# Turning the attention probabilities with VectorE and a trip through DRAM instead of on TensorE, in a decoder block on one core

## The chip, the core and the metric

The kernel runs on one core of one Trainium2 chip. The core has TensorE (PE in the profile: products, and PEld: loading of the stationary operand), VectorE (DVE), ScalarE (ACT), GpSimd (POOL), the queue of SyncE (SP) that issues nearly all transfers, and 16 DMA engines that carry them. Products land in PSUM, eight banks of 128 x 512 float32. The metric is the time of one execution on the device in microseconds (us), as the median of several executions.

## The reference, cut to what matters

One layer for 256 tokens of width 1024: a SwiGLU feed-forward, a mixing layer of two branches, a second SwiGLU feed-forward, a norm. The change lies in the mixing layer, between the softmax and the branch projections:

```python
n = rmsnorm(h, mix_norm[l])
z = n @ w_in[l]                                  # q, k, v (8 heads of 64) and two gMLP parts of 512
p_own = softmax(logits)                          # causal, 256 keys: one block holds the sequence
attn = einsum('bhqp,bhpd->bhqd', p_own, v_own)   # probabilities times values, by head
y_attn = attn @ w_branch_attn[l]
y_gmlp = gm @ w_branch_gmlp[l]                   # gm: spatial gating of the other branch
gates = sigmoid(n @ w_gate[l] + b_gate[l])       # 2048 columns
merged = gates[..., :D] * y_attn + gates[..., D:] * y_gmlp
h = h + merged @ w_out[l]
```

## The kernel before, in words

Activations lie with features on the partitions and the 256 tokens along the row. Each float32 weight is split into a high and a low part (`split`, lines 211 to 215: ScalarE casts, L212, VectorE subtracts, L214), and each product runs as high x both parts of the activation (L162, 512 columns) and low x high (L167, 256 columns). Weights arrive in halves of 512 KB, `raw`, in a ring of seven; SP issues the load of a half as soon as VectorE's subtraction has freed the slot seven halves earlier (L137). The split weights `w` lie in a ring of four units. A unit is split three units ahead of its use.

TensorE and SP keep the order of the code. The order of VectorE and ScalarE is set by a scheduler outside the few stretches that are marked by hand; the stretch of this change is not marked.

After the projections of q, k and the gMLP part come the scores. TensorE computes them for the two query tiles j of 128 tokens (`sc`, L586), then the spatial products of the gMLP branch (`mix`, L571, which read `gv` as stationary operand), and goes on without a break to sixteen gate blocks f = 0 to 15 (`gate_block`; the title of the change counts blocks from 1). Each is 16 products of 512 columns and 8 of 256 into one bank `pgate`; `collect` (lines 202 to 209) then copies the right half to `lo` on ScalarE (L205) and adds it to the left on VectorE (L209, output `gz`), which frees the bank. Under the gate blocks VectorE and ScalarE do the softmax of both query tiles: maxima (L596), exponentials with sums (L601), reciprocals (L604), products with the reciprocal (L606). The probabilities `prob[0]` and `prob[1]` lie with queries on the partitions, in the tile that the profile calls `mixed`; for products with the values the keys must be on the partitions.

`turn` (called behind f = 7 and f = 10, each for four heads) does that on TensorE: twelve transposes of 128 x 128 against the identity (`pk`, L634 to L636), copied from PSUM to `pT` by ScalarE (L640, two) and VectorE (L642, one). `attend` (behind f = 10 and f = 13, two head pairs each) multiplies with the values (`po`, L651 and L653) and splits the result into `aoT` for the branch projection (`pb`, L198 to L200), which begins after f = 15. Under the first four blocks `gated` finishes the gMLP branch: L659 adds the bias to a `mix` bank, L662 multiplies, and `split` writes `gmT`.

The eight banks are handed out in a row that the program fixes when it is built: gate block f takes a bank whose earlier owner must have been read out, and TensorE waits on that reader.

Later in the kernel, at L715, L723 and L727, the residual `h` is already turned as the change now turns the probabilities: VectorE transposes squares of 32 (`squares`), four transfers of 256 KB write them to DRAM (`hd`), two of 512 KB bring them back (`ht`).

Of the kernel before, what the change touches and what calls it, by code (L numbers as in the profile page):

```python
# [10 lines left out]
F32 = mybir.dt.float32  # L11
# [7 lines left out]
P = 128  # L19
D = 1024  # L20
S = 256
NT = S // P
DFF = 2816
KB = D // P
FB = DFF // P
HEADS = 8
HD = 64
# [16 lines left out]
def block_kernel(ctx, tc, t, out):  # L44
    nc = tc.nc
# [4 lines left out]
    act = ctx.enter_context(tc.tile_pool(name="act", bufs=1))  # L50
    tmp = ctx.enter_context(tc.tile_pool(name="tmp", bufs=2))
    small = ctx.enter_context(tc.tile_pool(name="small", bufs=4))
    psum = ctx.enter_context(tc.tile_pool(name="psum", bufs=8, space=PSUM))
    dram = ctx.enter_context(tc.tile_pool(name="dram", bufs=1, space=bass.MemoryType.DRAM))

    def bank(name):
        return psum.tile([P, 512], F32, tag="ps", name=name)
# [3 lines left out]
    h = act.tile([P, KB, S], F32, tag="h", name="h")  # L61
# [15 lines left out]
    ident = consts.tile([P, P], F32, name="ident")  # L77
# [133 lines left out]
    def split(hi, lo, src, later=False):  # L211
        nc.scalar.copy(hi, src)  # L212
        def rest():
            nc.vector.tensor_sub(lo, src, hi.bitcast(F32))  # L214
        return rest if later else rest()

    def alloc_T(name, tags):

        return [act.tile([P, 4, 2, S], F32R, tag=tag, name=f"{name}{c}") for c, tag in enumerate(tags)]
# [170 lines left out]
    def products(i0, nT, name, f, gu=None, ahead=ALONE):  # L390
        if gu is None:
            gu = tmp.tile([P, 2, S], F32, tag="gu", name=f"gu{name}{f}")
        w = unit(i0 + f, ahead)
        ps = [bank(f"{name}{'gu'[i]}{f}") for i in range(2)]
        by_passes([(ps[i], weights_of(w, nT, i)) for i in range(2)])
        for i in range(2):
            collect(gu[:, i, :], ps[i])
        return gu
# [50 lines left out]
    first = act.tile([P, 4, 2, S], F32, tag="nD", name="first")  # L449
# [3 lines left out]
    ps = {(f, i): bank(f"f1_{f}{i}") for f, i in at}  # L453
# [59 lines left out]
    with in_order():  # L513
# [6 lines left out]
        mix_a, mix_b = mixed[:, :FB], mixed[:, FB:]  # L520
        gates = mix_a[:, :2 * KB, :]
        gv = mix_a[:, 2 * KB:2 * KB + 4, :].rearrange("p (j a) t -> p j (a t)", j=NT)
        va = mix_b[:, 0:4, :].rearrange("p (j a) t -> p j (a t)", j=NT)
# [5 lines left out]
        prob = [mix_b[:, 8:12, :].rearrange("p a (b n) -> p (a b) n", b=2), mix_b[:, 12:20, :]]  # L529
# [36 lines left out]
    def spatial(ps, gp):  # L566

        for j in range(NT):
            for a in range(2):
                g = 2 * gp + a  # L570
                nc.tensor.matmul(ps[a * HD:(a + 1) * HD, j * P:(j + 1) * P],  # L571
                                 gv[:, j, g * HD:(g + 1) * HD], wsT[:, g, :], start=True, stop=True)


    for j in range(NT):
        n = (j + 1) * P
        per = 512 // n
        pr = prob[j]
        pr2 = pr.rearrange("p (a two) n -> p a two n", two=2)
        for a0 in range(0, HEADS // 2, per):  # L580

            pair = [bank(f"sc{j}{a0}{two}") for two in range(2)]
            for a in range(per):
                for two in range(2):
                    r = slice(two * HD, (two + 1) * HD)
                    nc.tensor.matmul(pair[two][:, a * n:(a + 1) * n], qT[r, a0 + a, j * P:(j + 1) * P],  # L586
                                     kT[r, a0 + a, :n], start=True, stop=True)
            for two in range(2):
                ps = pair[two].rearrange("p (a n) -> p a n", a=per)
                to = pr2[:, a0:a0 + per, two, :]  # L590
                if j:
                    nc.scalar.copy(to[:, :, :n - P], ps[:, :, :n - P])
                nc.vector.tensor_add(to[:, :, n - P:], ps[:, :, n - P:],
                                     mask[:, None, :].to_broadcast([P, per, P]))
        mx = small.tile([P, HEADS], F32, tag="mx", name=f"mx{j}")
        nc.vector.tensor_reduce(mx, pr, axis=AX.X, op=ALU.max)  # L596
        nm = small.tile([P, HEADS], F32, tag="nm", name=f"nm{j}")
        nc.vector.tensor_scalar(nm, mx, -(HD ** -0.5), None, op0=ALU.mult)
        sm = small.tile([P, HEADS], F32, tag="sm", name=f"sm{j}")
        for hd in range(HEADS):  # L600
            nc.scalar.activation(pr[:, hd, :], pr[:, hd, :], AF.Exp, bias=nm[:, hd:hd + 1],  # L601
                                 scale=HD ** -0.5, accum_out=sm[:, hd:hd + 1])
        ri = small.tile([P, HEADS], F32, tag="ri", name=f"ri{j}")
        nc.vector.reciprocal(ri, sm)  # L604
        for hd in range(HEADS):
            nc.vector.tensor_scalar(pr[:, hd, :], pr[:, hd, :], ri[:, hd:hd + 1], None, op0=ALU.mult)  # L606


    mix = []
    for pair in range(2):  # L610
        ps = bank(f"mix{pair}")
        for q in range(2):
            mix.append(ps[:, q * S:(q + 1) * S])
            spatial(mix[-1], 2 * pair + q)

    def gate_block(f):
        gz = tmp.tile([P, S], F32, tag="s", name=f"gz{f}")
        collect(gz, by_weights(f"pgate{f}", mg + f // 2, nT2, f % 2))  # L620
        nc.vector.tensor_mul(gz, gz, rows2)
        nc.scalar.activation(gates[:, f, :], gz, AF.Sigmoid, bias=bgate[:, f:f + 1])

    aoT, gmT = alloc_T("ag", ("nC", "nD"))

    def turn(first):

        hps = range(first, first + 2)
        pk0, pk1 = [bank(f"pk0{hp}") for hp in hps], bank(f"pk1{first}")
        for hp in hps:  # L630
            for a in range(2):
                hd, c1 = 2 * hp + a, (2 * (hp - first) + a) * P
                ps = pk0[hp - first]
                nc.tensor.transpose(ps[:, a * S:a * S + P], prob[0][:, hd, :], ident)  # L634
                nc.tensor.transpose(ps[:, a * S + P:a * S + S], prob[1][:, hd, :P], ident)
                nc.tensor.transpose(pk1[:, c1:c1 + P], prob[1][:, hd, P:], ident)  # L636
        t0 = []
        for hp, ps in zip(hps, pk0):
            t0.append(tmp.tile([P, 512], F32, tag="hg", name=f"pT0{hp}"))
            nc.scalar.copy(t0[-1], ps)  # L640
        t1 = tmp.tile([P, 512], F32, tag="gu", name=f"pT1{first}")
        nc.vector.tensor_copy(t1, pk1)  # L642
        return {hp: (t0[q], t1[:, q * S:(q + 1) * S]) for q, hp in enumerate(hps)}

    def attend(hp, t0, t1):

        po = bank(f"po{hp}")
        for a in range(2):
            hd = 2 * hp + a
            r = slice(a * HD, (a + 1) * HD)  # L650
            nc.tensor.matmul(po[r, :S], va[:, 0, hd * HD:(hd + 1) * HD], t0[:, a * S:(a + 1) * S],  # L651
                             start=True, stop=False)
            nc.tensor.matmul(po[r, P:S], va[:, 1, hd * HD:(hd + 1) * HD], t1[:, a * P:(a + 1) * P],  # L653
                             start=False, stop=True)
        split(aoT[:, hp, 0, :], aoT[:, hp, 1, :], po[:, :S])

    def gated(gp):
        m = tmp.tile([P, NT, P], F32, tag="s", name=f"mixb{gp}")
        nc.vector.tensor_add(m, mix[gp].rearrange("p (j i) -> p j i", j=NT),  # L659
                             bs[:, gp:gp + 1, :].to_broadcast([P, NT, P]))  # L660
        m2 = tmp.tile([P, S], F32, tag="us", name=f"gm{gp}")
        nc.vector.tensor_mul(m2, m.rearrange("p j i -> p (j i)"), uT[:, gp, :])  # L662
        split(gmT[:, gp, 0, :], gmT[:, gp, 1, :], m2)


    for f in range(2 * KB):
        gate_block(f)
        if f < 4:
            gated(f)
        if f == 7:  # L670
            turned = turn(0)
        elif f == 10:
            for hp in range(2):
                attend(hp, *turned[hp])
            turned = turn(2)
        elif f == 13:
            for hp in range(2, 4):
                attend(hp, *turned[hp])


    mT = alloc_T("mg", ("nA", "nB"))
    for f in range(KB):
        i = mb + 2 * (f // 4)
        ps = bank(f"pb{f}")
        c = slice(f % 4 * P, (f % 4 + 1) * P)
# [14 lines left out]
    with in_order():  # L700
# [3 lines left out]
        first = act.tile([P, 3, 2, S], F32, tag="nA", name="first2")  # L704
        gu = [products(f2, nT3, "f2", f, first[:, f]) for f in range(2)]
# [11 lines left out]
    hd = dram.tile([S, D], F32, name="hd")  # L717
# [117 lines left out]
```

## Time and profile before

| what | value |
|---|---|
| median of 3 runs | 538.11 us (538.0 to 538.14) |
| the profiled execution | 538.72 us, of it 536.8 us in the span of the profile |
| busy over the span | PE 98%, PEld 86%, DVE 76%, ACT 56%, POOL 3% |
| DMA engines | 59% busy, 194 GB/s |
| gate blocks to the first branch product (251.02 to 301.59 us) | PE 50.57 us of 50.57, DVE 42.84, ACT 38.50, DMA share 0.49 |

A busy share says only that instructions ran; what bounds a stretch is read from the waits and from the chain that ended last. A product's recorded duration is longer than its distance from the next one, because products overlap in the array: what a group costs TensorE is read from the distance between starts. In the timeline a row stands for a run of like instructions: its start, how long the run took, the engine, the line, the operation and the count; what stands in brackets is idle time ahead of it.

### The profile page before, as it was taken

What the parts mean: (1) busy time and instruction counts of PE and PEld (TensorE: products, weight loads), DVE (VectorE), ACT (ScalarE), POOL (GpSimd) and SP (SyncE); (2) the same over time, 40 slices, a digit from 0 to 9 for tenths busy, and PEclk for the clock granted to TensorE, in tenths of its full rate; (3) what the DMA queues carried; (4) which work ended last, traced back from release to release, by engine and by line L of the source; (5) the groups of instructions that cost most, each with busy time, mean ns of one, the idle gap of its engine ahead of it and who ended that gap; (6) DMA issues with size and microseconds to landing.
All of it is one profiled execution on the core that took longest, in us unless ns stands there. A gap on an engine that the chain in (4) does not pass through costs nothing.

```text
span 536.8 us, 8141 instructions
## 1 busy us (share of the span) xinstructions
PE 528.8 (98%) x3049; PEld 463.5 (86%) x3049; DVE 405.9 (76%) x682; ACT 303.0 (56%) x534; POOL 17.7 (3%) x23
## 2 busy tenths in 40 slices
PE   8999999999999999999999999999999999999995
PEld 7888888888888888888888998888888888888884
DVE  6799998788443689978897787799898878854324
ACT  7768566565433367447886544476657656553402
POOL 0040000000000001000000000001000000000002
PEclk9999999999999999999999999999999999999998
DMA  8985765657756329764266545259588765565002
GB/s 319 396 286 178 253 224 187 197 195 218 230 170 203 103 86 322 258 210 147 80 196 203 172 135 182 96 174 315 165 268 292 235 197 197 178 214 177 20 1 79
DMA packets 31287, 104.10 MB, mean 194 GB/s; under 512 B 3472, under 2 KB 6032, under 8 KB 31248
## 3 DMA queue, kind: packets, MB, share of 16 engines
q1 hardware_dynamic: 30960, 103.25, 58.2%
q8 instruction: 24, 0.39, 0.3%
q10 hardware_dynamic: 288, 0.33, 0.2%
q14 instruction: 15, 0.12, 0.1%
HBM read 101.47 MB, written 2.10 MB: 193 GB/s over the span
## 4 chain that ended last, share of the span: by engine, by line
PE 97%; DMA 1%; DVE 0%; issue 0%; ACT 0%; POOLq 0%; DVEq 0%; POOL 0%; ACTq 0%
PE acc L162 10%; PE f2u L162 7%; PE f2g L162 7%; PE f1u L162 7%; PE f1g L162 7%; PE pgate L162 6%; PE acc L167 5%; PE f2u L167 4%; PE f2g L167 4%; PE f1u L167 4%; PE f1g L167 4%; PE acch L200 4%; PE acch L198 4%; PE acch L199 4%; PE pgate L167 3%; PE pq L162 3%
## 5 line engine op out<-in xcount | busy, mean ns | idle before, releaser
L214 DVE TENSOR_TENSOR w<-raw,w 128x1024 fp32r<-128x1024 f32 x180 | 219.3, 1238 | 53.4 <-ACT w L212 53.0
L212 ACT CAST w<-raw 128x1024 fp32r<-128x1024 f32 x180 | 181.8, 1057 | 59.3 <-PE acc L167 21.2
L162 PE MATMUL f2g<-n,w 128*128 128x512 f32 x176 | 68.8, 391 | 0.0
L162 PE MATMUL f2u<-n,w 128*128 128x512 f32 x176 | 68.8, 391 | 0.0
L162 PE MATMUL f1g<-n,w 128*128 128x512 f32 x160 | 62.6, 391 | 0.0
L162 PE MATMUL f1u<-n,w 128*128 128x512 f32 x160 | 62.5, 391 | 0.0
L162 PE MATMUL acc<-f1h,w 128*128 128x512 f32 x176 | 43.4, 391 | 0.0
L167 PE MATMUL f2u<-n,w 128*128 128x256 f32 x176 | 43.2, 283 | 0.0
L167 PE MATMUL f2g<-n,w 128*128 128x256 f32 x176 | 43.0, 282 | 0.0
L167 PE MATMUL f1u<-n,w 128*128 128x256 f32 x160 | 39.2, 283 | 0.0
L167 PE MATMUL f1g<-n,w 128*128 128x256 f32 x160 | 39.1, 282 | 0.0
L162 PEld LDWEIGHTS f2u<-n,w 128*128 128x128 f32 x176 | 33.1, 188 | 6.3
L162 PEld LDWEIGHTS f2g<-n,w 128*128 128x128 f32 x176 | 33.1, 188 | 6.1
L162 PEld LDWEIGHTS acc<-f1h,w 128*128 128x128 f32 x176 | 31.9, 188 | 5.8
L162 PEld LDWEIGHTS f1u<-n,w 128*128 128x128 f32 x160 | 30.1, 188 | 5.7
L162 PEld LDWEIGHTS f1g<-n,w 128*128 128x128 f32 x160 | 30.1, 188 | 5.6
L167 PEld LDWEIGHTS f2u<-n,w 128*128 128x128 f32 x176 | 33.7, 191 | 0.9
L167 PEld LDWEIGHTS f2g<-n,w 128*128 128x128 f32 x176 | 33.6, 191 | 0.9
L162 PE MATMUL pgate<-n,w 128*128 128x512 f32 x128 | 33.1, 396 | 0.0
L199 PE MATMUL acch<-w,f2h 128*128 128x512 f32 x84 | 32.7, 389 | 0.0
L200 PE MATMUL acch<-w,f2h 128*128 128x512 f32 x84 | 32.7, 389 | 0.0
L198 PE MATMUL acch<-w,f2h 128*128 128x512 f32 x84 | 32.7, 389 | 0.0
(191 smaller groups left out, 933.0 us busy)
## 6 DMA issues: line engine op xcount, KB each, us to landing
raw<-in_f SPq DMA_DIRECT2D x84, 512.0 KB, 5.1
raw<-in_f1d SPq DMA_DIRECT2D x22, 512.0 KB, 4.4
raw<-in_f2d SPq DMA_DIRECT2D x22, 512.0 KB, 3.9
raw<-in_gate SPq DMA_DIRECT2D x16, 512.0 KB, 4.6
raw<-in_qk SPq DMA_DIRECT2D x8, 512.0 KB, 5.4
raw<-in_out SPq DMA_DIRECT2D x8, 512.0 KB, 4.4
front<-in_first SPq DMA_DIRECT2D x7, 384.0 KB, 5.9
raw<-in_v SPq DMA_DIRECT2D x4, 512.0 KB, 4.5
```

The lines of the kernel that those rows point to most:

```text
L162: nc.tensor.matmul(ps, st, both.rearrange("p two n -> p (two n)"), start=first, stop=last)
L167: nc.tensor.matmul(ps[:, n:], st, both[:, 0, :], start=False, stop=False)
L198: nc.tensor.matmul(ps, sh, mh, start=first, stop=False)
L199: nc.tensor.matmul(ps, sh, ml, start=False, stop=False)
L200: nc.tensor.matmul(ps, sl, mh, start=False, stop=last)
L212: nc.scalar.copy(hi, src)
L214: nc.vector.tensor_sub(lo, src, hi.bitcast(F32))
```

## The change

The twelve-by-two transposes on TensorE and their copies go. The code of the spatial products moves ahead of the softmax, since `turned[0]` takes over the space of `gv`, which those products read; TensorE's order of scores, spatial products and gate block 0 stays. Behind the multiplication with the reciprocals, VectorE turns the probabilities in squares of 32, for all eight heads in one instruction of 128 x 256: four for query tile 0, eight for query tile 1. A square has its keys on 32 partitions then, but in the wrong band of partitions; `to_keys` (behind f = 1) writes them to DRAM by key with eight transfers, four of 128 KB and four of 256 KB, in runs of 1 KB, and `by_keys` (behind f = 4) reads three blocks of 128 keys back with 512 KB each, over the place of the probabilities. `attend` for all four head pairs stands behind f = 12; its moving operand is no longer a contiguous row but 8 (or 4) runs of 32 columns, 256 columns apart.

```diff
     for j in range(NT):
...
+        turned.append(mix_a[:, 2 * KB:2 * KB + 4, :] if j == 0 else
+                      act.tile([P, KB, S], F32, tag="nC", name="turned1"))
+        for kb in range(n // 32):
+            nc.vector.transpose(turned[j][:, kb, :].rearrange("p (h c) -> p h c", c=32),
+                                pr[:, :, kb * 32:(kb + 1) * 32])
...
-    def turn(first):
...
-                nc.tensor.transpose(ps[:, a * S:a * S + P], prob[0][:, hd, :], ident)
-                nc.tensor.transpose(ps[:, a * S + P:a * S + S], prob[1][:, hd, :P], ident)
-                nc.tensor.transpose(pk1[:, c1:c1 + P], prob[1][:, hd, P:], ident)
...
-            nc.scalar.copy(t0[-1], ps)
...
-        nc.vector.tensor_copy(t1, pk1)
...
+    gmT, = alloc_T("gm", ("nD",))
+    on_way = [dram.tile([(j + 1) * P, 4, S], F32, name=f"on_way{j}") for j in range(NT)]
+
+    def to_keys(j):
+
+        for b in range(4):
+            nc.sync.dma_start(on_way[j][:, b, :].rearrange("(k r) n -> r k n", r=32),
+                              turned[j][32 * b:32 * (b + 1)])
+
+    def by_keys():
+
+
+        for j, t0, b0 in ((0, 0, 8), (1, 0, 12), (1, 1, 16)):
+            nc.sync.dma_start(mix_b[:, b0:b0 + 4, :], on_way[j][t0 * P:(t0 + 1) * P])
...
-            nc.tensor.matmul(po[r, :S], va[:, 0, hd * HD:(hd + 1) * HD], t0[:, a * S:(a + 1) * S],
+            r, c = slice(a * HD, (a + 1) * HD), slice(hd * 32, (hd + 1) * 32)
+            nc.tensor.matmul(po[r, :S], va[:, 0, hd * HD:(hd + 1) * HD], mix_b[:, 8:16, c],
...
+            nc.tensor.matmul(po[r, P:S], va[:, 1, hd * HD:(hd + 1) * HD], mix_b[:, 16:20, c],
...
-        if f == 7:
-            turned = turn(0)
-        elif f == 10:
-            for hp in range(2):
-                attend(hp, *turned[hp])
-            turned = turn(2)
-        elif f == 13:
-            for hp in range(2, 4):
-                attend(hp, *turned[hp])
+        if f == 1:
+            for j in range(NT):
+                to_keys(j)
+        elif f == 4:
+            by_keys()
+        elif f == 12:
+            aoT, = alloc_T("ao", ("nC",))
+            for hp in range(4):
+                attend(hp)
```

VectorE under the first gate blocks, before: from the softmax of query tile 1 to the collect of gate block 1 (`gz1`). Numbers behind names are buffers; `w47` is the weight unit of gate blocks 8 and 9.

```order
L606 TENSOR_SCALAR mixed_2086<-mixed_2086,ri1_2581 128x256 x8
L209 TENSOR_TENSOR gz0_2611<-pgate0_2612,lo_2638 128x256
L659 TENSOR_TENSOR mixb0_2643<-mix0_2591,bs_1495 128x256
L621 TENSOR_TENSOR gz0_2611<-gz0_2611,rowsb2_2163 128x256
L662 TENSOR_TENSOR gm0_2645<-mixb0_2643,mixed_2086 128x256
L214 TENSOR_TENSOR w47_2680<-raw47_0_2338,w47_2680 128x4x256
L209 TENSOR_TENSOR gz1_2649<-pgate1_2650,lo_2667 128x256
```

The same place after (line numbers of the changed kernel), from the softmax of query tile 0:

```order
L618 TENSOR_SCALAR mixed_2086<-mixed_2086,ri0_2576 128x128 x8
L624 STREAM_TRANSPOSE mixed_2086<-mixed_2086 128x256 x4
L616 RECIPROCAL ri1_2603<-sm1_2594 128x8
L618 TENSOR_SCALAR mixed_2086<-mixed_2086,ri1_2603 128x256 x8
L209 TENSOR_TENSOR gz0_2625<-pgate0_2626,lo_2652 128x256
L624 STREAM_TRANSPOSE turned1_2613<-mixed_2086 128x256 x8
L632 TENSOR_TENSOR gz0_2625<-gz0_2625,rowsb2_2163 128x256
L664 TENSOR_TENSOR mixb0_2657<-mix0_2545,bs_1495 128x256
L214 TENSOR_TENSOR w47_2702<-raw47_0_2338,w47_2702 128x4x256
L667 TENSOR_TENSOR gm0_2659<-mixb0_2657,mixed_2086 128x256
L214 TENSOR_TENSOR w47_2702<-raw47_1_2408,w47_2702 128x4x256
L214 TENSOR_TENSOR gm0_2622<-gm0_2659,gm0_2622 128x256
L209 TENSOR_TENSOR gz1_2663<-pgate1_2664,lo_2681 128x256
```

Four transposes stand ahead of the second reciprocal; eight stand between the collects of gate blocks 0 and 1, and a subtraction of `w47` and one of `gm0` have also come ahead of `gz1`. In both programs gate block 7 takes the bank of gate block 1, so TensorE can't start it before that collect.

The queue of SP, before: loads of the weight halves (`ba` and `bg` are the branch projections).

```order
L137 DMA raw50_0_2620<-in_gate 128x1024
L137 DMA raw50_1_2683<-in_gate 128x1024
L137 DMA raw51_0_2687<-in_ba 128x1024
L137 DMA raw51_1_2750<-in_ba 128x1024
L137 DMA raw52_0_2754<-in_bg 128x1024
```

After:

```order
L137 DMA raw50_0_2634<-in_gate 128x1024
L641 DMA on_way0_2623<-mixed_2086 32x4x256 x4
L641 DMA on_way1_2624<-turned1_2613 32x8x256 x4
L137 DMA raw50_1_2705<-in_gate 128x1024
L137 DMA raw51_0_2709<-in_ba 128x1024
L137 DMA raw51_1_2772<-in_ba 128x1024
L137 DMA raw52_0_2776<-in_bg 128x1024
L648 DMA mixed_2086<-on_way0_2623 128x1024
L648 DMA mixed_2086<-on_way1_2624 128x1024 x2
L137 DMA raw52_1_2830<-in_bg 128x1024
```

The eight writes stand ahead of the second half of unit 50 (gate blocks 14 and 15) and wait for VectorE's transposes; the three reads stand ahead of the second half of unit 52 and wait for the writes to land.

## Rows read from the trace of the kernel before

**Rows 1.** The page: its first line, TensorE's clock in 40 slices, and the chain that ended last by engine.

```profile
span 536.8 us, 8141 instructions
...
PEclk9999999999999999999999999999999999999998
...
PE 97%; DMA 1%; DVE 0%; issue 0%; ACT 0%; POOLq 0%; DVEq 0%; POOL 0%; ACTq 0%
```

**Rows 2.** Who waited for whom, TensorE alone, over the whole span: us in total, times, longest.

```profile
PE warm L92 <- DVE zeros L89: 1.2, 1, 1.2
PE f L191 <- ACT n L421: 0.4, 1, 0.4
```

**Rows 3.** Timeline of TensorE's weight loads from gate block f = 6 to f = 8, with the first group of transposes between f = 7 and f = 8. The loads of L167 mark the same point in each gate block.

```profile
269.31 1.13 PEld L167 LDWEIGHTS pgate<-n,w 128*128 128x128 f32 x8
270.36 1.70 PEld L162 LDWEIGHTS pgate<-n,w 128*128 128x128 f32 x8
272.10 1.13 PEld L167 LDWEIGHTS pgate<-n,w 128*128 128x128 f32 x8
273.16 0.19 PEld L162 LDWEIGHTS pgate<-n,w 128*128 128x128 f32 x1
273.29 0.14 PEld L634 LDWEIGHTS pk<-ident,mixed 128*128 128x128 f32 x1
...
274.71 1.46 PEld L162 LDWEIGHTS pgate<-n,w 128*128 128x128 f32 x7
276.21 1.13 PEld L167 LDWEIGHTS pgate<-n,w 128*128 128x128 f32 x8
```

**Rows 4.** The same view from f = 10 to f = 11, with four heads' products and the second group of transposes between them.

```profile
281.79 1.13 PEld L167 LDWEIGHTS pgate<-n,w 128*128 128x128 f32 x8
...
283.29 0.20 PEld L651 LDWEIGHTS po<-pT,mixed 128*64 128x64 f32 x4 [0.24 <-issue]
...
284.79 0.14 PEld L634 LDWEIGHTS pk<-ident,mixed 128*128 128x128 f32 x1 [0.17 <-issue]
...
286.05 1.45 PEld L162 LDWEIGHTS pgate<-n,w 128*128 128x128 f32 x7
287.54 1.13 PEld L167 LDWEIGHTS pgate<-n,w 128*128 128x128 f32 x8
```

**Rows 5.** The same view from f = 13 to f = 14, with the other four heads' products between them.

```profile
293.13 1.13 PEld L167 LDWEIGHTS pgate<-n,w 128*128 128x128 f32 x8
...
294.62 0.20 PEld L651 LDWEIGHTS po<-pT,mixed 128*64 128x64 f32 x4 [0.25 <-issue]
...
296.12 1.46 PEld L162 LDWEIGHTS pgate<-n,w 128*128 128x128 f32 x7 [0.17 <-issue]
297.62 1.13 PEld L167 LDWEIGHTS pgate<-n,w 128*128 128x128 f32 x8
```

**Rows 6.** Groups of instructions by line and shape: count, busy us in all and mean ns of one, idle us ahead of them.

```profile
L167 PE MATMUL pgate<-n,w 128*128 128x256 f32 x128 | 17.8, 282 | 0.0
...
L640 ACT COPY pT<-pk 128x512 f32<-128x512 f32 x4 | 2.2, 583 | 0.0
...
L191 PE MATMUL f<-n,w 128*128 128x256 f32 x8 | 2.0, 431 | 0.4 <-ACT n L421 0.4
...
L642 DVE COPY pT<-pk 128x512 f32<-128x512 f32 x2 | 1.4, 689 | 0.0
```

**Rows 7.** Timeline of VectorE under gate blocks 2 to 5: the end of the softmax and the collects of gate blocks 0 and 1 (the two rows of L209).

```profile
260.50 0.20 DVE L604 RECIPROCAL ri<-sm 128x8 f32<-128x8 f32 x1 [2.40 <-ACT mixed L601]
260.74 2.19 DVE L606 TENSOR_SCALAR mixed<-mixed,ri 128x256 f32<-128x256 f32 x8
262.85 0.42 DVE L209 TENSOR_TENSOR gz<-pgate,lo 128x256 f32<-128x256 f32 x1
263.18 0.41 DVE L659 TENSOR_TENSOR mixb<-mix,bs 128x256 f32<-128x256 f32 x1
...
264.18 1.22 DVE L214 TENSOR_TENSOR w<-raw,w 128x1024 fp32r<-128x1024 f32 x1
265.31 0.42 DVE L209 TENSOR_TENSOR gz<-pgate,lo 128x256 f32<-128x256 f32 x1
```

**Rows 8.** Timeline of VectorE later in the kernel, where it turns squares of 32 of `h`: input of 8 runs of 32 elements, 256 apart.

```profile
370.77 0.76 DVE L715 STREAM_TRANSPOSE squares<-h 128x256 f32<-128x256 f32 x2
371.46 0.65 DVE L383 TENSOR_TENSOR first<-first,rowsb 128x512 f32<-128x512 f32 x1
```

**Rows 9.** Transfers. Timeline of SP's queue where it issues the writes to `hd`; then, from the views of the single lines, the issue of the four writes (ns min/median/max) with the us to their landing, the us to landing of the two reads `ht`, and that of all weight halves (L137); last, SP's row of seven loads of gate weights.

```profile
386.50 3.06 SPq L723 DMA_DIRECT2D hd<-squares  x4
...
L723 SPq DMA_DIRECT2D hd<-squares x4: 333/624/1337, 386.5 to 388.2; - x4
...
DMA to landing us min/median/max: 2.9/4.2/5.2
...
DMA to landing us min/median/max: 5.5/6.0/6.4
...
DMA to landing us min/median/max: 3.6/4.8/12.0
...
237.85 27.90 SPq L137 DMA_DIRECT2D raw<-in_gate  x7
```

**Rows 10.** Busy time of each engine from gate block 0 to the first branch product: PE, PEld, DVE, ACT, POOL (with instructions), granted clock, DMA share, GB/s.

```profile
251.02:301.59 50.57, 50.57 (x314) 44.05 (x312) 42.84 (x88) 38.50 (x90) 0.00 (x0) 1.00 0.49 156
```

More of the change, by code (lines that the diff above doesn't have):

```diff
@@ L594, in block_kernel @@
                                      mask[:, None, :].to_broadcast([P, per, P]))
+    mix = []
+    for pair in range(2):
+        ps = bank(f"mix{pair}")
+        for q in range(2):
+            mix.append(ps[:, q * S:(q + 1) * S])
+            spatial(mix[-1], 2 * pair + q)
+    turned = []
+    for j in range(NT):
+        n, pr = (j + 1) * P, prob[j]
         mx = small.tile([P, HEADS], F32, tag="mx", name=f"mx{j}")
@@ L606, in block_kernel @@
             nc.vector.tensor_scalar(pr[:, hd, :], pr[:, hd, :], ri[:, hd:hd + 1], None, op0=ALU.mult)
[L609 to L614, printed above, removed]
+        turned.append(mix_a[:, 2 * KB:2 * KB + 4, :] if j == 0 else
[3 more added lines that the diff above has]
+                                pr[:, :, kb * 32:(kb + 1) * 32])
     def gate_block(f):
@@ L622, in gate_block, with attend @@
         nc.scalar.activation(gates[:, f, :], gz, AF.Sigmoid, bias=bgate[:, f:f + 1])
-    aoT, gmT = alloc_T("ag", ("nC", "nD"))
-    def turn(first):
[L628 to L633, printed above, removed]
-                nc.tensor.transpose(ps[:, a * S:a * S + P], prob[0][:, hd, :], ident)
-                nc.tensor.transpose(ps[:, a * S + P:a * S + S], prob[1][:, hd, :P], ident)
-                nc.tensor.transpose(pk1[:, c1:c1 + P], prob[1][:, hd, P:], ident)
-        t0 = []
-        for hp, ps in zip(hps, pk0):
-            t0.append(tmp.tile([P, 512], F32, tag="hg", name=f"pT0{hp}"))
-            nc.scalar.copy(t0[-1], ps)
-        t1 = tmp.tile([P, 512], F32, tag="gu", name=f"pT1{first}")
-        nc.vector.tensor_copy(t1, pk1)
-        return {hp: (t0[q], t1[:, q * S:(q + 1) * S]) for q, hp in enumerate(hps)}
-    def attend(hp, t0, t1):
+    gmT, = alloc_T("gm", ("nD",))
[7 more added lines that the diff above has]
+            nc.sync.dma_start(mix_b[:, b0:b0 + 4, :], on_way[j][t0 * P:(t0 + 1) * P])
+    def attend(hp):
         po = bank(f"po{hp}")
@@ L649, in attend @@
             hd = 2 * hp + a
-            r = slice(a * HD, (a + 1) * HD)
-            nc.tensor.matmul(po[r, :S], va[:, 0, hd * HD:(hd + 1) * HD], t0[:, a * S:(a + 1) * S],
+            r, c = slice(a * HD, (a + 1) * HD), slice(hd * 32, (hd + 1) * 32)
+            nc.tensor.matmul(po[r, :S], va[:, 0, hd * HD:(hd + 1) * HD], mix_b[:, 8:16, c],
                              start=True, stop=False)
-            nc.tensor.matmul(po[r, P:S], va[:, 1, hd * HD:(hd + 1) * HD], t1[:, a * P:(a + 1) * P],
+            nc.tensor.matmul(po[r, P:S], va[:, 1, hd * HD:(hd + 1) * HD], mix_b[:, 16:20, c],
                              start=False, stop=True)
@@ L669, in block_kernel @@
             gated(f)
-        if f == 7:
-            turned = turn(0)
-        elif f == 10:
-            for hp in range(2):
-                attend(hp, *turned[hp])
-            turned = turn(2)
-        elif f == 13:
-            for hp in range(2, 4):
-                attend(hp, *turned[hp])
+        if f == 1:
+            for j in range(NT):
+                to_keys(j)
[5 more added lines that the diff above has]
+                attend(hp)
     mT = alloc_T("mg", ("nA", "nB"))
```

## The prediction

> **What bounds the kernel now.** I read the chain that ended last first, then TensorE's waits, then the stretch of the change. [...] From gate block 0 to the first branch product it is busy for 50.57 of 50.57 us, beside 42.84 us of VectorE and a DMA share of 0.49 [rows 10]. So a microsecond of work taken off TensorE there shortens the kernel by as much, as long as nothing that feeds TensorE comes later than TensorE now asks for it; and work put on VectorE or the DMA engines costs nothing until it is late at one of TensorE's waits.
>
> **What leaves TensorE.** In undisturbed gate blocks the loads of L167 stand 272.10 - 269.31 = 2.79 us apart [rows 3]. Across the first group of transposes they stand 276.21 - 272.10 = 4.11 apart: it costs 1.32 us, 0.11 for each of twelve (the recorded durations overlap). Across four heads' products and the second group it is 287.54 - 281.79 = 5.75, so 2.96 more than a block [rows 4]; across the other four heads' products 297.62 - 293.13 = 4.49, so 1.70 more [rows 5]. Together 1.32 + 2.96 + 1.70 = 5.98 us. What stays is the products of eight heads in one group. Two groups by their own cost are 2 x 1.70 = 3.40; of each, some 0.4 is the switch in and out (the idle times of 0.25 and 0.17 in rows 5), and a joined group has that once, which gives 3.0. [...] The gain on TensorE is then 5.98 - 3.2 = **2.8 us**, 2.6 to 3.0 between the ends.
>
> The transposes' copies go too: 4 x 0.583 us of ScalarE and 2 x 0.689 of VectorE [rows 6]. Neither engine ends the chain, so this is worth nothing by itself.
>
> By rows 3 a transpose of 128 x 128 costs 0.11 us of the one engine that never waits; by rows 8 VectorE turns twice as many elements in 0.345 us, on an engine with idle time. [...]
>
> **What the products cost.** Their number and shapes stay, but the moving operand is read in runs of 32 columns. No row shows TensorE streaming so. The nearest is VectorE, which read the same shape of runs at L715: two in 371.46 - 370.77 = 0.69 us [rows 8], as fast as its contiguous rows, 263.18 - 262.85 = 0.33 each [rows 7]. A gain is excluded, since the columns stay as many. For the upper end I take the slowest 256-column product of the trace against the usual one, 431 against 282 ns, 1.53 times [rows 6]; that one met data as it arrived. The ends are +0 and +0.53 x 3.2 = +1.7 us; I take 0, by the nearer row. [...]
>
> **What VectorE gets.** Twelve transposes at 0.345 us (rows 8) are 4.1 us, less 1.4 of copies. Four of them come behind the first softmax multiplication, in the 2.40 us in which VectorE waited for the second softmax [rows 7]: 1.4 us, hidden. The other eight come between the collects of gate blocks 0 and 1, and that is **the close place**: gate block 7 uses the bank of gate block 1. From the start of `gz0` at 262.85 to `gz1`, by the order after and the distances of rows 7: `gz0` 0.33; eight transposes 2.76; two small ones 0.66; `w47` 1.13; `gm0` 0.33; `w47` 1.13; the low part of `gm0` 0.33. The sum is 6.67, so `gz1` starts at 269.52 instead of 265.31 and ends at 269.94. TensorE began block 7 one load after 270.36, at 270.57 [rows 3]. So 0.63 us are left. If nothing overlapped (0.42 for each small instruction and transpose, 1.22 for each half of a weight) the sum is 0.42 x 13 + 2 x 1.22 = 7.90, `gz1` ends at 271.17, and TensorE waits 0.60. I take no wait; the distances are measured. ScalarE's two casts of `w47` are unmoved ahead of this, so VectorE need not wait for it. Behind `gz1` there is more room: `gz2` comes after four small instructions and a half of a weight, at 269.52 + 4 x 0.33 + 1.13 = 271.97, done by 272.4, and block 9 needs its bank at 270.57 + 2 x 2.79 = 276.15.
>
> **What SP gets.** The writes wait for the last transpose, at 262.85 + 0.33 + 2.76 + 0.08 = 266.0. I count eight issues as the four of rows 9 twice, 6 us at the most, but those for query tile 0 are free from 260 on; so the last are out by 266.0 + 3.06 = 269.1, and land by 269.1 + 5.2 = 274.3. Queued behind them is first the second half of unit 50. Before, SP issued the last gate load by 237.85 + 27.90 = 265.75 [rows 9]; now some 4 us later, for gate block 14, which began at 296.12 [rows 5]. The slowest load of the trace took 12.0 us to land, so this costs nothing. The reads stand behind the first half of unit 52, whose slot is freed by the second half of `w48`, at 271.97 + 4 x 0.33 + 1.2 = 274.5, when the writes have landed: issued by 275.8, landed by 275.8 + 6.4 = 282.2. TensorE comes to the products behind f = 12 at 270.57 + 6 x 2.79 = 287.31. That leaves **5.1 us**; with the slowest landing of the trace, 12.0, the data come at 287.8 and TensorE waits 0.5. The traffic grows by 3 MB on 156 GB/s x 50.57 us = 7.9 MB, so the share of 0.49 becomes about 0.68, and the loads have the slack named above. I count nothing. The branch projection asks for the split results three gate blocks later, where it had two.
>
> **The sum.** The profiled execution took 538.72 us, 536.8 in its span. Less 2.8 the span is 534.0. The median of the runs is 538.11, 0.61 below the profiled one, and the change lies in the middle of the span, so I take the same 2.8 from it: **535.3 us**.
>
> **Rivals.**
>
> *VectorE is late at gate block 7.* For it: VectorE is the busiest engine beside TensorE, and 0.63 us is little. Against it: the distances are measured, on the same shape. Without overlap TensorE loses 0.6 us; if a turn of probabilities took as long as the copies of 512 columns (0.69, rows 6), eight would add 2.76, `gz1` would end at 272.7 and TensorE wait 2.1. This gives 535.9 to 537.4.
>
> *The trip through DRAM comes back late.* The price is 0.5 us at the slowest landing seen: 535.8. Only a landing of 15 us would undo the gain.
>
> *The products read their runs slowly* — the case that can end slower than before. It decides from 3.2 + 2.8 = 6.0 us for the joined group, 1.9 times; at 1.53 times the time is 537.0. Three times the price, beyond all rows, gives 535.3 + 6.4 = 541.7. Against it: rows 8, though of another engine.
>
> [...]
>
> **How the numbers follow.** A measurement of this kernel can tell some 0.2%, 1.1 us, from no change: faster means below 537.0. Forecast 0.70, with its own range 535.0 to 535.8. VectorE late 0.12, of which 0.10 ends below 537.0. Late data 0.05, faster still. Slow products 0.08: 0.02 within 0.2% and 0.06 slower. Crawling writes 0.02, slower. What I have not thought of 0.03, within 0.2%. So faster 0.70 + 0.10 + 0.05 = 0.85, same 0.02 + 0.02 + 0.03 = 0.07, slower 0.08. The range runs from 534.9 (3.0 us of gain and a little scatter of the runs) to 537.0, the upper end of the products' bound; it leaves out the 0.15 above it.
>
> **What the profile after would show.** Right: no rows of L634 to L636, a distance of 2.79 us between the L167 loads of f = 7 and 8 and of f = 10 and 11, some 6.0 us once between f = 12 and 13, and still no wait of TensorE. A wait ahead of f = 7 released by `gz` would show VectorE late; idle time ahead of `po` released by a transfer, the trip late; starts of `po` further apart than 0.09 us on average without a wait, slow products. The prediction is wrong if the transposes of the probabilities run further apart than 0.42 us, or if TensorE loses the time again at a later stage.

## The result, and the profile after

The changed kernel takes **534.78 us** (median of 6 runs, 534.65 to 535.1) against 538.22 for the kernel before, run on the same chip (538.0 to 538.5): ratio 0.9936, 95% interval 0.9923 to 0.9949. That is 3.4 us faster. The forecast was 535.3, with 534.9 as the lower end of its range: right in direction, with a gain of 2.8 us that was too small, and 0.12 us beyond the end of the range.

The profiled execution of the changed kernel took 534.82 us, 533.1 in its span. From its page, the first line, TensorE's granted clock in 40 slices and the chain by engine, as [rows 1]:

```profile
span 533.1 us, 8126 instructions
...
PEclk9999999999999999999999999999999999999999
...
PE 97%; DMA 1%; DVE 0%; issue 0%; ACT 0%; POOLq 0%; DVEq 0%; POOL 0%; ACTq 0%
```

Its waits of TensorE (us in total, times, longest), as [rows 2]:

```profile
PE warm L92 <- DVE zeros L89: 1.2, 1, 1.2
PE f L191 <- ACT n L421: 0.4, 1, 0.4
```

TensorE still bounds the kernel and has no new wait. Engines by window from gate block 0 to the first branch product (columns as in [rows 10]):

```profile
250.46:298.06 47.60, 47.60 (x289) 41.61 (x288) 45.12 (x97) 36.11 (x85) 0.00 (x0) 1.00 0.69 221
```

The stretch took 50.57 us before and takes 47.60: **2.97 us**, all of it TensorE's time. VectorE and the DMA engines do more in a shorter time (DMA share 0.69, forecast 0.68), and neither is waited for. Where [rows 3] and [rows 4] had transposes, TensorE's weight loads now follow each other undisturbed; the products come once, behind f = 12. A gate block is eight products of 512 columns and eight of 256, as the counts show (x8 and x8), not sixteen and eight as the description of the kernel before has it. Timeline of the weight loads:

```profile
268.75 1.13 PEld L167 LDWEIGHTS pgate<-n,w 128*128 128x128 f32 x8
269.80 1.70 PEld L162 LDWEIGHTS pgate<-n,w 128*128 128x128 f32 x8
271.54 1.13 PEld L167 LDWEIGHTS pgate<-n,w 128*128 128x128 f32 x8
...
285.50 1.13 PEld L167 LDWEIGHTS pgate<-n,w 128*128 128x128 f32 x8
...
287.00 0.20 PEld L656 LDWEIGHTS po<-mixed 128*64 128x64 f32 x4 [0.24 <-ACT w L212]
...
287.60 0.30 PEld L656 LDWEIGHTS po<-mixed 128*64 128x64 f32 x4
...
288.25 0.30 PEld L656 LDWEIGHTS po<-mixed 128*64 128x64 f32 x4
...
289.80 1.46 PEld L162 LDWEIGHTS pgate<-n,w 128*128 128x128 f32 x7 [0.17 <-DVE gz L209]
291.30 1.13 PEld L167 LDWEIGHTS pgate<-n,w 128*128 128x128 f32 x8
```

From f = 6 to f = 7 it is 271.54 - 268.75 = 2.79, and 2.79 to 2.81 wherever no products stand. Across the products it is 291.30 - 285.50 = 5.80, 3.01 over a block. The idle time ahead of `po` is 0.24 us, as it was in [rows 4], and the pairs of heads are 0.65 apart. So 1.32 + 2.96 + 1.70 = 5.98 us went and 3.01 came back.

The new work of VectorE, answering [rows 7], and of SP's queue, answering [rows 9]; two timelines:

```profile
257.64 1.43 DVE L624 STREAM_TRANSPOSE mixed<-mixed 128x256 f32<-128x256 f32 x4
259.92 0.20 DVE L616 RECIPROCAL ri<-sm 128x8 f32<-128x8 f32 x1 [0.85 <-ACT mixed L613]
...
262.60 2.71 DVE L624 STREAM_TRANSPOSE turned<-mixed 128x256 f32<-128x256 f32 x8
...
268.82 0.41 DVE L209 TENSOR_TENSOR gz<-pgate,lo 128x256 f32<-128x256 f32 x1
```

```profile
259.09 1.97 SPq L641 DMA_DIRECT2D on_way<-mixed  x4
265.34 3.03 SPq L641 DMA_DIRECT2D on_way<-turned  x4
268.47 1.18 SPq L137 DMA_DIRECT2D raw<-in_gate  x1
...
274.27 1.38 SPq L648 DMA_DIRECT2D mixed<-on_way  x3
```

The first four turns fill part of the wait for the second softmax (0.85 us are left of 2.40). The collect of gate block 1 ends at 268.82 + 0.41 = 269.23, and TensorE's first own load of block 7 is one load after 269.80, at 270.01: 0.78 us to spare, 0.63 forecast. From the view of the reads' line (L648), their us from issue to landing (min, median, max):

```profile
DMA to landing us min/median/max: 6.8/7.6/8.7
```

The last of them went out by 275.2, so the data are there by 283.9 at the latest, 3.1 us ahead of the products.

The stretch explains 2.97 of the 3.44 us between the medians. The other 0.47 lie outside it, and the experiments show where most of them are.

### The profile page after: what moved, and what is told of

It is laid out like the page before. It is cut to its first block, busy times and chain, and to the rows that moved or that the text cites. A ratio compares the mean times of both kernels' runs of the same rounds, so it can differ in the third digit from the quotient of the medians.

```text
span 533.1 us, 8126 instructions
## 1 busy us (share of the span) xinstructions
PE 525.2 (99%) x3025; PEld 460.4 (86%) x3025; DVE 408.3 (77%) x692; ACT 300.7 (56%) x530; POOL 18.5 (3%) x23
## 4 chain that ended last, share of the span: by engine, by line
PE 97%; DMA 1%; DVE 0%; issue 0%; ACT 0%; POOLq 0%; DVEq 0%; POOL 0%; ACTq 0%
PE acc L162 10%; PE f2u L162 8%; PE f2g L162 8%; PE f1u L162 7%; PE f1g L162 7%; PE pgate L162 6%; PE acc L167 5%; PE f2u L167 4%; PE f2g L167 4%; PE f1u L167 4%; PE f1g L167 4%; PE acch L200 4%; PE acch L199 4%; PE acch L198 4%; PE pgate L167 3%; PE pq L162 3%
## 5 line engine op out<-in xcount | busy, mean ns | idle before, releaser
L167 PE MATMUL f2u<-n,w 128*128 128x256 f32 x176 | 43.2, 283 | 0.0
L167 PE MATMUL f2g<-n,w 128*128 128x256 f32 x176 | 43.0, 282 | 0.0
L167 PE MATMUL f1u<-n,w 128*128 128x256 f32 x160 | 39.2, 283 | 0.0
L167 PE MATMUL f1g<-n,w 128*128 128x256 f32 x160 | 39.1, 282 | 0.0
L167 PEld LDWEIGHTS f2u<-n,w 128*128 128x128 f32 x176 | 33.7, 191 | 0.9
L167 PEld LDWEIGHTS f2g<-n,w 128*128 128x128 f32 x176 | 33.6, 191 | 0.9
```

The source lines that it names most:

```text
L167: nc.tensor.matmul(ps[:, n:], st, both[:, 0, :], start=False, stop=False)
```

## Experiments

**The two kernels again.** Both were run unchanged, for a second profile of each.

> The kernel before, unchanged, profiled a second time. It prices the scatter of a profiled execution. Theory 1 (the change saves 2.97 us in its stage, and the remaining 0.5 us between the medians is how soon the granted clock rises at the start of an execution, which the change doesn't touch): ratio 1.000 within 0.001, gate block 0 begins between 250.4 and 251.1 us after the span's start, and the stretch from gate block 0 to the first branch product takes 50.55 to 50.60 us again. Theory 2 (the change brings the 0.5 us elsewhere): gate block 0 begins at 251.0 again, within 0.1.

> The changed kernel, unchanged, profiled a second time. Theory 1: 534.8 us within 0.4; the stretch from gate block 0 to the first branch product 47.6 us again within 0.05, while the time at which gate block 0 begins differs from the first profile's 250.46 by some tenths. Theory 2: gate block 0 begins at 250.5 again, within 0.1, so that a difference of 0.56 us to the kernel before stands in each pair of profiles.

Measured: the kernel before 538.32 us median, ratio 0.9999 (0.9990 to 1.0007); the changed one 534.84, ratio 0.9940 (0.9927 to 0.9953). TensorE's first products, from the timelines of the kernel before again, of the changed kernel's first profile, and of its second:

```profile
5.25 1.34 PE L191 MATMUL f<-n,w 128*128 128x256 f32 x8 [0.48 <-ACT n L421]
```

```profile
5.21 1.27 PE L191 MATMUL f<-n,w 128*128 128x256 f32 x8 [0.43 <-ACT n L421]
```

```profile
5.33 2.08 PE L191 MATMUL f<-n,w 128*128 128x256 f32 x8 [0.56 <-ACT n L421]
```

These eight products take 1.3 us in some executions of either kernel and 2.1 in others; where they took 2.1, the next ones can be slow as well (the four of L167 behind them took 1.05 us in the run with the products in one group, further down, 0.64 where the eight took 1.27). Gate block 0 began at 250.50 in the kernel before again, at 250.46 in the first profile of the changed one and at 252.38 in the second, whose execution took 536.73 us. So the start differs by execution, while the stretch of the change took 50.57 us and 47.60 again in the second profiles. By their times most executions of both kernels begin without the longest delay (28 of the 29 of the kernel before that ran beside these lie within 0.8 us of each other, 5 of 6 of the changed one within 0.6). A late start of some tenths can hide in that scatter, so the medians alone don't tell how much of their difference is the start's; two profiles that began alike settle it. In the first profiles of the two kernels, where the eight products took 2.04 and 1.27 us, the granted clock is recorded as 1.00 from the first half us to 12 us. So these profiles show no such rise of the clock as theory 1 names, and what sets the pace there stays open.

The kernel before again (538.17 us) and the first profile of the changed one (534.82) started alike, and their 3.35 us can be laid out: 0.04 to gate block 0, 50.57 - 47.60 = 2.97 in the stretch of the change, and 0.34 behind it. Neither theory had that. The 0.34 lie in the last 10 us, on VectorE; timelines of the kernel before again, then of the changed one, at the last half row of the norm:

```profile
529.86 0.42 DVE L348 SCALAR_TENSOR_TENSOR ht<-endh,ht 128x256 f32<-128x256 f32 x1 [0.53 <-PE endh L200]
530.78 0.48 DVE L745 CUSTOM_DVE_ANT_0 sq<-ht,ms 128x256 bf16<-128x256 f32 x1 [0.50 <-DVE ht L348]
...
532.70 0.35 ACTq L766 DMA_DIRECT2D out_dram<-o  x1
```

```profile
526.86 0.42 DVE L348 SCALAR_TENSOR_TENSOR ht<-endh,ht 128x256 f32<-128x256 f32 x1 [0.53 <-PE endh L200]
527.43 0.48 DVE L750 CUSTOM_DVE_ANT_0 sq<-ht,ms 128x256 bf16<-128x256 f32 x1
...
529.34 0.35 ACTq L771 DMA_DIRECT2D out_dram<-o  x1
```

The square `sq` starts 0.92 us after `ht` in the one and 0.57 in the other. What stands in brackets before is VectorE's own last instruction; the profile names no other engine and no transfer for the square. In the second profile of the changed kernel it is 0.57 too, and 0.93 in the profile that the prediction used. Everything behind the square, the last transfer too, waits for it: that transfer is issued 532.70 - 530.78 = 1.92 and 529.34 - 527.43 = 1.91 us after the square's start. From the issue of that transfer to the end of the execution it is 538.17 - 532.70 = 5.47 and 534.82 - 529.34 = 5.48, so the 0.35 us count in full.

**Ten more instructions on VectorE.** The change makes VectorE's program ten instructions longer (twelve transposes, less two copies). The same can be had in the kernel before without the change:

```diff
         gate_block(f)
+        if f == 9:
+            ten = small.tile([P, 10], F32, tag="ten", name="ten")
+            for i in range(10):
+                nc.vector.tensor_copy(ten[:, i:i + 1], rows2[:, i:i + 1])
```

The scheduler put the ten copies between 213.7 and 228.6 us, some 300 us ahead of the square.

> The kernel before with ten copies of one column (128 x 1) more on VectorE, among the work ahead of the scores, where TensorE ends the chain; nothing reads them. The change also makes VectorE's program ten instructions longer (twelve transposes more, two copies fewer). In three profiles without these ten VectorE pauses 0.50 us ahead of the last square of the norm, with its inputs in hand; in three with them it doesn't, and the kernel's last transfer goes out 0.35 us sooner. Theory A (the pause hangs on where that instruction lies in VectorE's program): the pause is gone here too, and the kernel is 0.35 us faster than before, 537.8 us, ratio 0.9993. Theory B (it hangs on something else that the change does): the pause stays, 538.15 us.

Timeline of VectorE at the same place:

```profile
529.69 0.42 DVE L348 SCALAR_TENSOR_TENSOR ht<-endh,ht 128x256 f32<-128x256 f32 x1 [0.53 <-PE endh L200]
530.26 0.48 DVE L749 CUSTOM_DVE_ANT_0 sq<-ht,ms 128x256 bf16<-128x256 f32 x1
```

The pause is gone (0.57 again), and the stretch of the change took 50.57 us as before: theory A. The median is 537.78 against 538.18. The ratio that is worked out from all executions, 1.0001 (0.9988 to 1.0013), can't show 0.4 us, because four of its twelve began slowly (539.46 to 539.90), as did four of 29 of the kernel before by their times (539.83 to 539.95). The other eight took 537.61 to 538.01, the other 25 of the kernel before 537.87 to 538.58.

The DMA view counts transfers of instructions too, and one of them stands close to the pause. In the kernel before again, from 531.0 to 531.5 us:

```profile
q14 instruction: 1, 0.01, 4.8%
```

In the profile that the prediction used, such a packet comes between 531.90 and 531.95 us, some 0.6 us after the square has started (531.31). This queue has 15 packets over the span in either kernel. In the first profile of the changed kernel, which has no pause, its last packet comes sooner, between 507.0 and 507.5 us; there VectorE only splits weights and stands idle for 3.08 us between them. Since the packet comes behind the pause, its landing is not what the square waited for. What VectorE does in the pause, and whether the packet has to do with it, is not shown. The runs show that the place in the program decides: the square starts 0.92 to 0.93 us after `ht` in the three profiles with 682 instructions on VectorE (two of the kernel before, and the next experiment), and 0.57 us after it in the seven programs with 692 or more. The pause costs 0.35 us where it falls on the chain that ends the kernel.

**The products in one group, without the rest of the change.** In the kernel before, `attend` moves behind f = 12 for all four pairs; the transposes stay on TensorE. The copies of the second group of transposes also go to other space (the part of the diff that is left out), since both groups' copies are now held at once.

```diff
...
-            for hp in range(2):
-                attend(hp, *turned[hp])
-            turned = turn(2)
-        elif f == 13:
-            for hp in range(2, 4):
+            turned.update(turn(2))
+        elif f == 12:
+            for hp in range(4):
```

> The kernel before with only one part of the change: the products of all four head pairs stand in one group behind f = 12, the transposes stay on TensorE (behind f = 7 and f = 10) with their copies. Theory 1: the joined group costs TensorE 3.01 us as in the changed kernel, where the two groups cost 3.40, so 0.39 us are gained: 537.8 us against 538.2, ratio 0.9993. The forecast's 3.2 for a joined group would give 0.2 us, ratio 0.9996. A rival: the gain of the joined group hangs on the moving operand's runs of 32, then nothing is gained here.

Measured: 538.19 us median, 537.73 the lowest; ratio 0.9997 (0.9988 to 1.0006), too wide for 0.4 us. The weight loads show it:

```profile
289.76 1.13 PEld L167 LDWEIGHTS pgate<-n,w 128*128 128x128 f32 x8
...
291.25 0.20 PEld L652 LDWEIGHTS po<-mixed 128*64 128x64 f32 x4 [0.24 <-issue]
...
295.55 1.13 PEld L167 LDWEIGHTS pgate<-n,w 128*128 128x128 f32 x8
```

The group costs 295.55 - 289.76 - 2.79 = 3.00 us with contiguous operands, so the 3.01 of the changed kernel hold no charge for runs of 32, and none ahead of the group's first product beyond the 0.24 idle of both. It saves 0.33 us: in the kernel before again the loads of f = 0 and f = 15 are 299.89 - 252.01 = 47.88 apart, here 301.14 - 253.59 = 47.55. That is 0.06 less than 3.40 - 3.01, since in [rows 4] the first group shared a switch with the transposes. Its VectorE program is as long as before, and its pause is there (0.50 us, the square 0.92 after `ht`).

**The transposes back, read by nobody.** In the changed kernel, TensorE transposes the values 24 times again; no copy follows.

```diff
+    def kept_turns(f):
+        to = [bank(f"kept{f}{i}") for i in range(3)]
+        for i in range(12):
+            c, s = i // 3 * P, i % 4 * P
+            nc.tensor.transpose(to[i % 3][:, c:c + P], va[:, i % 2, s:s + P], ident)
...
+        elif f in (7, 10):
+            kept_turns(f)
```

> The changed kernel with 24 transposes of 128 x 128 back on TensorE, twelve behind f = 7 and twelve behind f = 10; they turn the values, and nothing reads them, so no copy and no wait hangs on them. Theory 1 (the change's gain is the transposes' time on TensorE plus one switch): 24 x 0.11 = 2.6 us more than the changed kernel, 537.4 us, ratio to the kernel before 0.9985. Theory 2 (part of the gain comes from the copies that left VectorE and ScalarE, or from a later or earlier supply): less of it comes back, under 2.2 us, 537.0 us or below.

Measured: 539.06 us, ratio 1.0022 (1.0012 to 1.0033), 4.2 us over the changed kernel: more than either theory. TensorE's waits, then its loads, then the collect that the wait names, here and in the first profile of the kernel before:

```profile
PE kept L655 <- DVE gz L209: 1.3, 1, 1.3
```

```profile
273.60 1.13 PEld L167 LDWEIGHTS pgate<-n,w 128*128 128x128 f32 x8
...
276.67 1.07 PEld L655 LDWEIGHTS kept<-ident,mixed 128*128 128x128 f32 x10 [1.53 <-issue]
...
279.22 1.13 PEld L167 LDWEIGHTS pgate<-n,w 128*128 128x128 f32 x8
...
284.81 1.13 PEld L167 LDWEIGHTS pgate<-n,w 128*128 128x128 f32 x8
...
288.92 1.13 PEld L167 LDWEIGHTS pgate<-n,w 128*128 128x128 f32 x8
```

```profile
276.14 0.42 DVE L209 TENSOR_TENSOR gz<-pgate,lo 128x256 f32<-128x256 f32 x1
```

```profile
272.38 0.43 DVE L209 TENSOR_TENSOR gz<-pgate,lo 128x256 f32<-128x256 f32 x1
```

The group behind f = 10 costs 288.92 - 284.81 - 2.79 = 1.32, the one behind f = 7 279.22 - 273.60 - 2.79 = 2.83. There TensorE asks for three banks at once, and the third still waits for a collect that VectorE's turns have made late: that of gate block 3 ends at 276.14 + 0.42 = 276.56, and TensorE goes on at 276.67. Counted from the start of gate block 0 (252.52 here, 251.02 in the kernel before) it ends after 24.04 us instead of 272.81 - 251.02 = 21.79. To separate the two, the same transposes were put behind f = 11 and f = 14:

> The changed kernel again with 24 unread transposes of the values on TensorE, now behind f = 11 and f = 14 instead of f = 7 and f = 10. Behind f = 7 the group of twelve had waited for a collect of VectorE (2.83 us over a block), behind f = 10 it cost 1.32. Theory 1 (the price of the transposes is 0.11 us each, the rest was the wait for the bank): no wait of TensorE here, each group 1.32 us over a block, 2.64 us more than the changed kernel, 537.5 us. Theory 2 (24 transposes cost some 4.2 us on TensorE however they stand): 539 us.

Measured: 537.47 us, ratio 0.9987 (0.9978 to 0.9996), no new wait of TensorE, 2.63 us over the changed kernel's 534.84. Its weight loads across the first group:

```profile
282.62 1.13 PEld L167 LDWEIGHTS pgate<-n,w 128*128 128x128 f32 x8
...
286.73 1.13 PEld L167 LDWEIGHTS pgate<-n,w 128*128 128x128 f32 x8
```

This group costs 286.73 - 282.62 - 2.79 = 1.32 us, and the second as much. So the transposes cost 0.11 us each, whether anything reads them or not, and 2 x 1.32 with the 0.33 of the joined group make the 2.97 of the stretch. The 1.5 us of the other run are the forecast's first rival, VectorE late at a bank, brought about by asking for banks sooner.

**Four turns twice.** This looks for the edge of the close place from VectorE's side.

```diff
-        for kb in range(n // 32):
+        for kb in list(range(n // 32)) + list(range(4 * j)):
```

> The changed kernel with four of the eight turns of query tile 1 done twice, between the collects of gate blocks 0 and 1: 4 x 0.334 = 1.34 us more of VectorE. In the changed kernel the collect of block 1 ended 0.78 us ahead of gate block 7. Theory (the forecast's close place): TensorE waits 1.34 - 0.78 = 0.56 us ahead of gate block 7, released by the collect gz, 535.4 us. Rival (the scheduler's other work gives way, or the slack is larger): no wait, 534.8.

Measured: 535.13 us, ratio 0.9941 (0.9929 to 0.9953), 0.29 over the changed kernel. Timelines of VectorE's collect and of TensorE's loads:

```profile
269.80 0.42 DVE L209 TENSOR_TENSOR gz<-pgate,lo 128x256 f32<-128x256 f32 x1
```

```profile
268.76 1.13 PEld L167 LDWEIGHTS pgate<-n,w 128*128 128x128 f32 x8
269.82 0.19 PEld L162 LDWEIGHTS pgate<-n,w 128*128 128x128 f32 x1
270.34 1.46 PEld L162 LDWEIGHTS pgate<-n,w 128*128 128x128 f32 x7 [0.32 <-ACT w L212]
271.83 1.13 PEld L167 LDWEIGHTS pgate<-n,w 128*128 128x128 f32 x8
```

The wait is there, at the place that was named: TensorE goes on 0.12 us after the collect ends at 270.22, and block 7 stands 0.28 us over a block. It is half of the expected 0.56, because the scheduler put one small subtraction (0.34) behind the collect, so `gz1` came 0.98 us later and not 1.34. The 0.98 less the 0.78 of slack, and 0.12 until TensorE goes on, make the 0.32 of idle time in the row. The row names a cast of ScalarE. That cast ended at 270.15, ahead of the collect, and in the run with the transposes back TensorE also went on 0.11 us behind a collect, so the collect fits better.

**Reads two blocks later.** In the changed kernel `by_keys()` stands behind f = 6 instead of f = 4.

> The changed kernel with the three reads behind f = 6 instead of f = 4. By the order of SP's queue they then stand behind the first load of unit 53, which went out by 282.6 us in the changed kernel; with 1.4 us of issue and 6.8 to 8.7 to land the data come at 290 to 292, where TensorE asked for them at 287.0. Theory (the trip is hidden only while its data come ahead of the products; in the changed kernel it had some 3 us left): TensorE waits 3 to 5 us ahead of the products, 538 to 540 us. Rival (the reads land sooner on a quiet queue, or the products wait for something else): under 536.

Measured: 537.42 us median (536.45 to 540.59, the profiled one 536.45), ratio 0.9987 (0.9972 to 1.0001). SP's queue, then TensorE's waits:

```profile
280.29 1.42 SPq L648 DMA_DIRECT2D mixed<-on_way  x3
```

```profile
PE po L658 <- DMA mixed<-on_way: 0.6, 1, 0.6
PE po L656 <- DMA mixed<-on_way: 0.4, 1, 0.4
```

TensorE waits for the transfers. The median is 2.6 us over the changed kernel; the profiled execution, the quickest of the eleven, is 1.6 over it, and there the group of products costs 4.57 us instead of 3.01. I expected 3 to 5, and that was too much: the reads stood behind one load of unit 53, not both, so they went out at 280.3 instead of 282.6, and they landed in 7.4 us at the most instead of 8.7. For the profiled execution the theory's sum comes out with these numbers: 6.0 us of delay, less 3.1 of slack, less 1.3 of quicker landing, are 1.6. The slower executions have no profile.

**The operand column by column.** Here the products read the same data in another order, each element 1 KB from the one before; the queries of a block come out in another order.

```diff
-            nc.tensor.matmul(po[r, :S], va[:, 0, hd * HD:(hd + 1) * HD], mix_b[:, 8:16, c],
+            nc.tensor.matmul(po[r, :S], va[:, 0, hd * HD:(hd + 1) * HD], mix_b[:, 8:16, c].rearrange("p a c -> p c a"),
...
-            nc.tensor.matmul(po[r, P:S], va[:, 1, hd * HD:(hd + 1) * HD], mix_b[:, 16:20, c],
+            nc.tensor.matmul(po[r, P:S], va[:, 1, hd * HD:(hd + 1) * HD], mix_b[:, 16:20, c].rearrange("p a c -> p c a"),
```

> The changed kernel with the moving operand of the products read one element of each run after another (the next element 1 KB away) instead of run by run; the queries of a block come out in another order, so the attention's result is permuted. Theory of the forecast (the way in which the operand lies costs TensorE nothing): distances of 0.65 us for each pair of heads' four products, the joined group 3.01 us, 534.8 us. [...]

Measured: 537.45 us, ratio 0.9987 (0.9978 to 0.9996), 2.6 over the changed kernel. The weight loads of the products:

```profile
286.92 0.20 PEld L656 LDWEIGHTS po<-mixed 128*64 128x64 f32 x4 [0.24 <-ACT w L212]
...
288.03 0.41 PEld L656 LDWEIGHTS po<-mixed 128*64 128x64 f32 x4
...
289.34 0.41 PEld L656 LDWEIGHTS po<-mixed 128*64 128x64 f32 x4
```

A pair of heads takes 289.34 - 288.03 = 1.31 us instead of 0.65, twice as long. The way in which the operand lies does matter, so the theory as I worded it is wrong; what costs nothing is reading in runs of 32: 0.65 us for a pair, as with contiguous operands (292.50 - 291.85 = 0.65 in the run with the products in one group).

## Why the prediction was right in direction and too small

*TensorE bounds the stretch; its saved time is the gain.* Right: 2.97 us over the stretch, and no new wait.

*The transposes, 1.32 us a group.* Right: put back unread, they cost 2.63 us.

*The joined products, 3.2 us.* This is the first term that failed. My own sum from the rows gave 3.0; the 0.2 on top was my estimate, and no run shows it: the group cost 3.01, with 0.24 idle ahead of it as before. The gain on TensorE was 2.97 instead of 2.8.

*"The change lies in the middle of the span, so I take the same 2.8".* This is the step that cost most. It put everything behind the stretch at no difference, and left out that ten instructions more on VectorE move every later instruction in its program. The pause ahead of the last square, 0.35 us on the chain that ends the kernel, was gone with them; the same ten without the change took it away too. The two terms together are 0.17 + 0.35 = 0.52 us, and 538.11 - 2.97 - 0.35 = 534.79. From the 538.22 of the runs beside the changed kernel 0.12 us stay over, which is within the scatter of the runs. The range stopped at 3.0 us of gain and had no room for the second term.

*Runs of 32 columns at no cost.* Right, and in part luck: the row behind it was one of VectorE and says nothing of TensorE. Reading by column would have cost 2.6 us, so the rival was a real one and decided by the order of reading.

*VectorE at gate block 7.* Right: 0.78 us left, 0.63 forecast. The rival was close, since 1.34 us more of turns bring the wait.

*The trip through DRAM.* Right that it is hidden. The reads took up to 8.7 us instead of 6.4, so 3.1 us were left and not 5.1. The eight writes landed in 2.1 to 4.6 us (view of line L641); no run shows the crawling writes to which the forecast gave 0.02.

*VectorE's turns against TensorE's transposes.* The twelve turns took 1.43 + 2.71 = 4.1 us, as forecast. On the chain that ended last they would have cost more than the 2.97 us that the stretch became shorter. They were hidden, since TensorE has no new wait and VectorE did not end the chain (DVE 0%).

## What to carry to other kernels

Where one engine is busy for the whole stretch, price what leaves it by the distances between its starts, and then count the slack of each engine and queue that takes the work over; here 0.8 us on VectorE and 3 us on the transfers decided. Don't add a charge that no row shows. And read the last chain of the kernel for pauses that nobody releases: one that depends on the length of an engine's program can go, or come, with an edit elsewhere. Here the kernel with 682 instructions on VectorE has one, worth 0.35 us, and that with ten more has none, so a range should leave room for it on both sides.

## What the runs showed of the hardware that I had not expected

- VectorE paused 0.50 us (0.35 more than elsewhere) between two instructions with all inputs in hand, and no longer did so there when ten unread instructions stood ahead of them. A transfer of instructions comes some 0.6 us behind the pause in the trace; why VectorE pauses stays open.
- A TensorE product of 64 rows of output took twice as long when its moving operand stepped 1 KB from element to element (1.31 instead of 0.65 us for a pair of heads), and no longer than a contiguous one when it came in runs of 32 float32.
- The first eight products of an execution took 1.3 or 2.1 us, in either kernel, with the granted clock recorded as 1.00; with the products right behind them, up to 1.9 us of the whole time hang on that. What sets their pace stays open.
